# Query, key and value projections of an attention layer merged into 512-column products

## The chip, the cores and the metric

The kernel runs on one core of one Trainium2 chip. The metric is the device time of one execution in microseconds. Engines are named as in the profile: PE (TensorE), DVE (VectorE), ACT (ScalarE), POOL (GpSimd), and SP's queue, which issues the transfers.

## What is computed

One inference step of a two-layer encoder trunk for 640 tokens (a prompt of 512, and 8 running streams of 16 new tokens each) with 1024 features. Layer 0 mixes tokens by gating and convolution, layer 1 by an attention with forget values and RMS-normed queries and keys; each is followed by a convolutional feed-forward network (FFN). The change lies in layer 1's attention:

```python
def _fox_project(x, w_in, b_f, q_norm, k_norm):
    z = x @ w_in
    q, k, v, f = jnp.split(z, [D_C, 2 * D_C, 3 * D_C], axis=-1)
    q = _rmsnorm(q.reshape(b, t, C_HEADS, C_HEAD_DIM), q_norm)
    k = _rmsnorm(k.reshape(b, t, C_HEADS, C_HEAD_DIM), k_norm)
    v = v.reshape(b, t, C_HEADS, C_HEAD_DIM)
    logf = jax.nn.log_sigmoid((f + b_f).astype(jnp.float32))
    return q, k, v, logf

def _fox_attend(q, k, v, dq, dk, q_pos, k_pos):
    s = jnp.einsum('bthd,bshd->bhts', q, k, preferred_element_type=jnp.float32) * (C_HEAD_DIM ** -0.5)
    s = s + jnp.swapaxes(dq, 1, 2)[..., :, None] - jnp.swapaxes(dk, 1, 2)[..., None, :]
    s = jnp.where(k_pos[None, :] <= q_pos[:, None], s, NEG_INF)
    p = jax.nn.softmax(s, axis=-1)
    return jnp.einsum('bhts,bshd->bthd', p.astype(v.dtype), v)
```

There are 16 heads of 64 features. The prompt attends to itself, each stream to 256 cached keys and its own 16. The outputs go through `w_out`. Keys and values are outputs of the step as well.

## The kernel before

Tokens and weights are float32. To keep that accuracy, every factor is split into a high and a low float32r part (`weights`, L88 and L89, for weights; `split` and `prep` for activations), and a product is three matmuls: high by high, low by high, high by low. The weights come in units of 128 x 1024 through a pool `wts` with three buffers each for the raw unit and its two parts.

In time, the stages are the first mixer (to some 220 us), FFN 0 (to 679.6 us), the attention (to 1039 us), the rest of its output projection with the next norm (to 1076 us) and FFN 1.

The attention works through four groups of four heads, each group as two pairs. For a group g, `project` (L484) makes queries, keys and values, tokens on partitions, in a z tile of five token blocks each. Per kind there are two weight units, and each token block takes 8 chunks x 3 matmuls of 256 columns (L507), two blocks side by side in one 512-column PSUM tile `pj` of a pool with two buffers. ACT evacuates each block with the token's norm factor (L510). For queries and keys, ACT squares (L515), DVE reduces to sums per head (L516), POOL takes the power -1/2 (`rstd_of`, L151 and L152), then DVE scales (L519, z x ss) and, for keys, multiplies by the norm's weights (L521). `decay` makes the forget values and their sums; it stands after the queries of group 0.

For each pair, `operands` (L537 to L552) transposes queries and keys on PE, and ACT and DVE make high and low parts of them, `qa` and `ka` with `qb` and `kb`; halves of these are copied by transfers on SP's queue (L545, L548). `prompt_block` takes 128 queries of one head: scores `sc` on PE (L569, L570), mask on DVE (L571), `softmax` (maximum on DVE, L589; exponential on ACT, L591; reciprocal and division on DVE, L592 and L594), transposes (L576), copies `u` (DVE L579, ACT L581) and value products `pv` (L583). Blocks 3 to 0 of both heads alternate; `streams_pair` (L634 to L670) is laid between them, four per group. The PSUM pools are pj 2, sc 2, pt 3 and pv 1 buffers. The output projection `po` of the first six (for blocks 6 and 7 of the output, four) head pairs uses the same two pj buffers and stands in the program behind the last group; for it, `split` makes `sh` and `sl` from the finished heads.

The order of instructions on each engine isn't that of the program. A list scheduler (`schedule_with_timeline_sim=True`) sets it when the kernel is built, from the program's order, the dependences, the rotation of the pools and its own estimates of durations. It takes projections of a later group between the attention work of an earlier one. What is shown below as the order is what it put out.

## Time and profile before

| what | value |
|---|---|
| median of 3 runs | 1533.6 us (1533.28 to 1536.43) |
| span of the profiled execution, first to last instruction | 1531.9 us |
| the profiled execution's own device time | not given by the page; the median is 1.7 us above its span |
| PE busy | 1517.8 us, 99%, 11008 matmuls |
| DVE busy | 899.1 us, 59% |
| ACT busy | 559.4 us, 37% |
| POOL busy | 237.4 us, 15% |
| mean granted clock of PE | 1.000 |
| HBM read and written | 125.41 and 11.54 MB |

"Busy" is the time in which an instruction of the engine ran; a matmul's recorded duration is longer than the distance to the next one's start, since matmuls are pipelined, so costs on PE are taken from distances of starts. The chain of waits is the work that ended last, followed back from the last instruction. A row of a group names line, engine and operation, output <- inputs, shape and count; behind the bar stand busy us and mean ns of one, then the engine's idle time before it and what ended it. A row of stretches gives busy us and count for each engine.

### The profile page before, as it was taken

What the parts mean: (1) busy time and instruction counts of PE and PEld (TensorE: products, weight loads), DVE (VectorE), ACT (ScalarE), POOL (GpSimd) and SP (SyncE); (2) the same over time, 40 slices, a digit from 0 to 9 for tenths busy, and PEclk for the clock granted to TensorE, in tenths of its full rate; (3) what the DMA queues carried; (4) which work ended last, traced back from release to release, by engine and by line L of the source; (5) the groups of instructions that cost most, each with busy time, mean ns of one, the idle gap of its engine ahead of it and who ended that gap; (6) DMA issues with size and microseconds to landing.
All of it is one profiled execution on the core that took longest, in us unless ns stands there. A gap on an engine that the chain in (4) does not pass through costs nothing.

```text
span 1531.9 us, 26648 instructions
## 1 busy us (share of the span) xinstructions
PE 1517.8 (99%) x11008; PEld 1473.5 (96%) x11008; DVE 899.1 (59%) x1541; ACT 559.4 (37%) x918; POOL 237.4 (15%) x281
## 2 busy tenths in 40 slices
PE   8999999999999999999999999999999999999999
PEld 6999999999999999999989888888999999999998
DVE  6545437644653655675676766768765466365463
ACT  5422334322322322345545454535432233133231
POOL 5000122201210201143111111003221021021010
PEclk9999999999999999999999999999999999999999
DMA  6222212222223222243544343523222222321313
GB/s 226 77 82 73 77 56 85 68 81 85 62 64 95 64 66 93 62 156 103 180 128 136 122 123 104 183 60 107 83 60 76 87 67 57 98 73 53 107 47 106
DMA packets 52296, 142.90 MB, mean 93 GB/s; under 512 B 6656, under 2 KB 13744, under 8 KB 52048
## 3 DMA queue, kind: packets, MB, share of 16 engines
q1 hardware_dynamic: 45424, 133.79, 28.6%
q10 hardware_dynamic: 6752, 7.41, 1.4%
q8 instruction: 87, 1.43, 0.4%
q14 instruction: 33, 0.27, 0.1%
HBM read 125.41 MB, written 11.54 MB: 89 GB/s over the span
## 4 chain that ended last, share of the span: by engine, by line
PE 96%; DVE 2%; issue 1%; ACT 1%; DMA 0%; POOL 0%; SPq 0%; DVEq 0%; ACTq 0%
PE mm L109 71%; PE pj L507 10%; PE pv L583 3%; PE po L109 2%; PE pt L576 1%; PE mm L239 1%; PE pt L662 1%; PE sc L569 1%; DVE hl L132 1%; PE sc L570 1%; DVE wlo L89 1%; PE scs L641 1%; PE pt L537 1%; PE pt L655 0%; PE scs L634 0%
## 5 line engine op out<-in xcount | busy, mean ns | idle before, releaser
L88 ACT CAST whi<-raw 128x1024 fp32r<-128x1024 f32 (+4 forms) x222 | 207.6, 937 | 494.6 <-PE mm L109 426.1
L109 PE MATMUL mm<-hl,whi 128*128 128x320 f32 x1664 | 379.4, 309 | 0.5 <-DVE hl L132 0.5
L109 PE MATMUL mm<-hh,whi 128*128 128x320 f32 x1664 | 379.8, 309 | 0.0
L109 PE MATMUL mm<-hh,wlo 128*128 128x320 f32 x1664 | 379.2, 309 | 0.0
L109 PEld LDWEIGHTS mm<-hl,whi 128*128 128x128 f32 x1664 | 278.2, 188 | 0.7 <-DVE hl L132 0.7
L109 PEld LDWEIGHTS mm<-hh,whi 128*128 128x128 f32 x1664 | 278.2, 188 | 0.1
L109 PEld LDWEIGHTS mm<-hh,wlo 128*128 128x128 f32 x1664 | 278.0, 188 | 0.0
L89 DVE TENSOR_TENSOR wlo<-raw,whi 128x1024 fp32r<-128x1024 f32 (+4 forms) x222 | 245.5, 1107 | 33.3 <-ACT whi L88 33.0
L109 PE MATMUL mm<-sh,wlo 128*128 128x320 f32 x866 | 197.2, 309 | 1.3 <-DVE wlo L89 1.3
L109 PE MATMUL mm<-sl,whi 128*128 128x320 f32 x866 | 197.2, 309 | 0.0
L109 PE MATMUL mm<-sh,whi 128*128 128x320 f32 x866 | 196.2, 309 | 0.0
L202 POOL COPY so<-zp 128x18 f32<-128x18 f32 x88 | 89.4, 1016 | 570.4 <-DVE zp L191 570.4
L190 DVE TENSOR_TENSOR zp<-mm,rb 128x512 f32<-128x512 f32 x88 | 60.9, 692 | 195.8 <-PE mm L109 195.8
L209 DVE TENSOR_TENSOR x<-mm,x 128x640 f32<-128x640 f32 x79 | 65.0, 823 | 185.6 <-PE mm L109 185.6
L198 DVE SCALAR_TENSOR_TENSOR t<-zp,cst,t 128x656 f32<-128x656 f32 x184 | 165.1, 900 | 10.3 <-ACT t L196 5.6
L109 PEld LDWEIGHTS mm<-sh,wlo 128*128 128x128 f32 x866 | 144.6, 188 | 1.6 <-DVE wlo L89 1.6
L109 PEld LDWEIGHTS mm<-sl,whi 128*128 128x128 f32 x866 | 144.8, 188 | 0.0
L109 PEld LDWEIGHTS mm<-sh,whi 128*128 128x128 f32 x866 | 144.4, 188 | 0.2 <-issue 0.2
L507 PE MATMUL pj<-wlo,hh 128*128 128x256 f32 x480 | 137.7, 287 | 0.7 <-DVE wlo L89 0.7
L507 PE MATMUL pj<-whi,hh 128*128 128x256 f32 x480 | 137.7, 287 | 0.0
L507 PE MATMUL pj<-whi,hl 128*128 128x256 f32 x480 | 137.5, 287 | 0.0
L507 PEld LDWEIGHTS pj<-wlo,hh 128*128 128x128 f32 x480 | 91.6, 191 | 2.8 <-issue 1.6
(188 smaller groups left out, 1691.3 us busy)
## 6 DMA issues: line engine op xcount, KB each, us to landing
...
```

What stands on the lines that cost most here:

```text
L88: nc.scalar.copy(out=hi[:, c], in_=raw[:, c])
L89: nc.vector.tensor_tensor(out=lo[:, c], in0=raw[:, c], in1=hi[:, c].bitcast(F32), op=ALU.subtract)
L109: nc.tensor.matmul(outs[h], lhsT=l, rhs=r[:, h * HT:(h + 1) * HT], start=start and k == 0, stop=stop and k == 2)
L132: nc.vector.scalar_tensor_tensor(out=lo, in0=x, scalar=gs, in1=hi.bitcast(F32), op0=ALU.mult, op1=ALU.subtract)
L190: nc.vector.tensor_tensor(out=op, in0=a[:, 0:TP], in1=b[:, 0:TP], op=ALU.mult)
L198: nc.vector.scalar_tensor_tensor(out=cv[:, 0:CW], in0=zp[:, i:i + CW], scalar=w[:, i:i + 1], in1=cv[:, 0:CW], op0=ALU.mult, op1=ALU.add)
L202: self.nc.gpsimd.tensor_copy(out=out.rearrange("p (s c) -> p s c", c=2), in_=zp[:, 496:ZW].rearrange("p (s c) -> p s c", c=18)[:, :, 16:18])
L209: self.nc.vector.tensor_tensor(out=x, in0=ps[:, C0:C0 + T], in1=x, op=ALU.add)
L239: nc.tensor.matmul(pvs[tb], lhsT=l[:, tb * P:(tb + 1) * P], rhs=r[:, (kc % 2) * 512:(kc % 2 + 1) * 512], start=kc == 0 and k == 0, stop=kc ...
L507: nc.tensor.matmul(out[tb], lhsT=l[:, tb * P:(tb + 1) * P], rhs=r[:, c:c + 256], start=kc == 0 and i == 0, stop=kc == 7 and i == 2)
L537: nc.tensor.transpose(t[:, tb * P:(tb + 1) * P], z[i][:, tb, pair * P:(pair + 1) * P], k.ident)
L583: nc.tensor.matmul(ov[64 * hh:64 * hh + 64, i * P:n], lhsT=z[2][:, j, (2 * pair + hh) * 64:(2 * pair + hh) * 64 + 64], rhs=u[:, j * P:(j + ...
```

## The change

Queries and keys of a group are projected together, 256 + 256 columns side by side (`project_qk`), and values for two groups at once (`project_v`, called for groups 0 and 2). Every projection matmul is now 512 columns wide and each token block takes a whole pj tile; there are four weight units for such a product instead of two. In group 0 the token blocks go in pairs over the weights, as before for queries only. `decay` comes after queries and keys of group 0. One z tile holds queries and keys: z x ss is one DVE instruction for both, and the key norm's product takes half of that tile. The pool of weights has four buffers for the split parts and three for the raw unit, as before; the square has one buffer. The constants `w_qk` and `w_vc` replace `w_c`, with the same bytes. Comments are dropped, and the scratch for dynamic DMAs is set.

```diff
-        self.wp = pool(ctx, "wts", bufs=3)
+        self.wp = pool(ctx, "wts", bufs=4)
...
-        raw = self.wp.tile([P, 1024], F32, tag="raw", name=self.nm("raw"))
+        raw = self.wp.tile([P, 1024], F32, tag="raw", name=self.nm("raw"), bufs=3)
...
-    def project(self, g, h, first, after_q=None):
+    def walk(self, us, n, h, pairs):
+        k, nc = self.k, self.nc
+        out = [None] * 5
+        for tbs in ([(0, 1), (2, 3), (4,)] if pairs else [(tb,) for tb in range(5)]):
+            for tb in tbs:
+                out[tb] = self.pj.tile([P, 512], F32, tag="pj", name=k.nm("pj"))
+            for kc in range(8):
+                wh, wl = us[kc // n]
+                hh, hl = h[kc]
+                c = (kc % n) * 512
+                for tb in tbs:
+                    for i, (l, r) in enumerate(((hh, wh), (hl, wh), (hh, wl))):
+                        nc.tensor.matmul(out[tb], lhsT=l[:, tb * P:(tb + 1) * P], rhs=r[:, c:c + 512],
+                                         start=kc == 0 and i == 0, stop=kc == 7 and i == 2)
+            for tb in tbs:
+                yield tb, out[tb]
+
+    def project_qk(self, g, h):
+        us = [k.weights(io["w_qk"][g, u]) for u in range(4)]
+        zt = self.zp.tile([P, 5, 512], F32, tag="qk", name=k.nm("z"), bufs=2)
+        ss = self.zp.tile([P, 40], F32, tag="ss", name=k.nm("ss"))
+        for tb, o in self.walk(us, 2, h, g == 0):
+            nc.scalar.activation(out=zt[:, tb, :], in_=o, func=AF.Copy, scale=self.rt[:, tb:tb + 1])
+            sq = self.zp.tile([P, 512], F32, tag="sq", name=k.nm("sq"), bufs=1)
+            nc.scalar.activation(out=sq, in_=zt[:, tb, :], func=AF.Square)
+            s = ss[:, tb * 8:tb * 8 + 8]
+            nc.vector.reduce_sum(out=s, in_=sq.rearrange("p (h d) -> p h d", d=64), axis=AX.X)
+            k.rstd_of(s, s, 1.0 / 64)
+        zh = zt.rearrange("p t (h d) -> p (t h) d", d=64)
+        nc.vector.tensor_tensor(out=zh, in0=zh, in1=ss.unsqueeze(2).broadcast_to([P, 40, 64]), op=ALU.mult)
+        zk = zt[:, :, 256:512].rearrange("p t (h d) -> p t h d", d=64)
+        nc.vector.tensor_tensor(out=zk, in0=zk, in1=self.cst[:, O_KN:O_KN + 64].unsqueeze(1).unsqueeze(1).broadcast_to([P, 5, 4, 64]), op=ALU.mult)
...
+        return zt[:, :, 0:256], zt[:, :, 256:512]
+
+    def project_v(self, gg, h):
+        us = [k.weights(io["w_vc"][gg, u]) for u in range(4)]
+        zt = self.zp.tile([P, 5, 512], F32, tag="v", name=k.nm("z"), bufs=2)
+        for tb, o in self.walk(us, 2, h, False):
+            nc.scalar.activation(out=zt[:, tb, :], in_=o, func=AF.Copy, scale=self.rt[:, tb:tb + 1])
...
+    v = []
     for g in range(4):
-        z = at.project(g, h, g == 0, decay if g == 0 else None)
+        qk = at.project_qk(g, h)
+        if g == 0:
+            decay()
+        if g % 2 == 0:
+            v += at.project_v(g // 2, h)
+        z = qk + (v[g],)
...
-    nc = bacc.Bacc("TRN2", target_bir_lowering=False, num_devices=1)
+    nc = bacc.Bacc("TRN2", target_bir_lowering=False, num_devices=1, dynamic_dma_scratch_size=1024)
```

The lines of the attention behind `project` move by six in the listing (L569 is L575 in the changed kernel, L546 is L552, L571 is L577, L109 stays).

The order of the instructions moves. Groups are counted from 0. DVE at the start of group 2, from the copy of the streams' keys to the mask of the first score; `qb` and `ka` are operands of group 2, the squares' sums `ss` and `z` belong to group 3. Before:

```order
L604 COPY kts_9141<-pt_9136 128x256
L89 TENSOR_TENSOR wlo_9891<-raw_9889,whi_9890 128x1024
L546 SCALAR_TENSOR_TENSOR qb_9165<-pt_9153,qn_6341,qa_9163 64x512
L549 TENSOR_TENSOR ka_9164<-pt_9158,ka_9164 64x512
L546 SCALAR_TENSOR_TENSOR qb_9177<-pt_9153,qn_6341,qa_9175 64x512
L549 TENSOR_TENSOR ka_9176<-pt_9158,ka_9176 64x512
L516 TENSOR_REDUCE ss_9862<-sq_9863 128x4
L516 TENSOR_REDUCE ss_9862<-sq_9868 128x4
L151 TENSOR_SCALAR ss_9862<-ss_9862 128x4 x2
L571 TENSOR_TENSOR sc_9188<-sc_9188,mskb 128x128
```

In the changed kernel:

```order
L610 COPY kts_8565<-pt_8560 128x256
L513 TENSOR_REDUCE ss_9170<-sq_9321 128x8
L151 TENSOR_SCALAR ss_9170<-ss_9170 128x8
L552 SCALAR_TENSOR_TENSOR qb_8589<-pt_8577,qn_6341,qa_8587 64x512
L516 TENSOR_TENSOR z_9169<-z_9169,ss_9170 128x2560
L555 TENSOR_TENSOR ka_8588<-pt_8582,ka_8588 64x512
L98 TENSOR_TENSOR sl_9342<-x_77,sh_9341 128x640
L552 SCALAR_TENSOR_TENSOR qb_8601<-pt_8577,qn_6341,qa_8599 64x512
L518 TENSOR_TENSOR z_9169<-z_9169,atcst 128x5x256
L555 TENSOR_TENSOR ka_8600<-pt_8582,ka_8600 64x512
L577 TENSOR_TENSOR sc_8612<-sc_8612,mskb 128x128
```

The scaling z x ss of group 3, now 128x2560, and the key norm's product stand between the operands of group 2's first pair; before, these four operands followed each other.

PE at the same place, from the transposes of group 2's operands (`pt` from `z`). Before, where 57 matmuls of the projection follow before the first score `sc`:

```order
L537 MATMUL pt_9158<-cst,z_8836 128x128 x4
L507 MATMUL pj_9734<-whi_9728,hl_6173 128x256
L507 MATMUL pj_9734<-wlo_9729,hh_6172 128x256
L507 MATMUL pj_9734<-whi_9728,hh_6218 128x256
L507 MATMUL pj_9734<-whi_9728,hl_6219 128x256
L507 MATMUL pj_9734<-wlo_9729,hh_6218 128x256
L507 MATMUL pj_9734<-whi_9728,hh_6264 128x256
```

In the changed kernel, to that score:

```order
L543 MATMUL pt_8577<-cst,z_8244 128x128 x4
L589 MATMUL pv_7970<-u_8216,z_6734 64x128
L543 MATMUL pt_8582<-cst,z_8244 128x128 x4
L109 MATMUL po_9944<-sl_9338,whi_9939 128x320
L109 MATMUL po_9945<-sl_9338,whi_9939 128x320
L109 MATMUL po_9944<-sh_9337,wlo_9940 128x320
L109 MATMUL po_9945<-sh_9337,wlo_9940 128x320
L109 MATMUL po_9944<-sh_9341,whi_9939 128x320
L109 MATMUL po_9945<-sh_9341,whi_9939 128x320
L575 MATMUL sc_8612<-ka_8588,qa_8587 128x512
L576 MATMUL sc_8612<-kb_8590,qb_8589 128x512
L640 MATMUL scs_8638<-sr,sl 128x272
```

Six matmuls of the output projection stand there now, and no projection of a later group: all of these come earlier in the changed order.

PE in the second pair of group 2, from the scores on: `pj` is the projection, `pt` transposes, `pv` value products, `sc` scores. Before:

```order
L507 MATMUL pj_10073<-wlo_10061,hh_6080 128x256
L655 MATMUL pt_9607<-cst,pp_9599 128x128 x2
L569 MATMUL sc_9652<-ka_9291,qa_9290 128x256
L570 MATMUL sc_9652<-kb_9293,qb_9292 128x256
L507 MATMUL pj_10073<-whi_10060,hh_6126 128x256
L655 MATMUL pt_9607<-cst,pn_6353 128x128
L569 MATMUL sc_9670<-ka_9303,qa_9302 128x256
L570 MATMUL sc_9670<-kb_9305,qb_9304 128x256
L507 MATMUL pj_10073<-whi_10060,hl_6127 128x256
L507 MATMUL pj_10073<-wlo_10061,hh_6126 128x256
L507 MATMUL pj_10073<-whi_10066,hh_6172 128x256
L507 MATMUL pj_10073<-whi_10066,hl_6173 128x256
```

In the changed kernel:

```order
L575 MATMUL sc_8826<-ka_8588,qa_8587 128x256
L576 MATMUL sc_8826<-kb_8590,qb_8589 128x256
L582 MATMUL pt_8749<-cst,p_8742 128x128 x3
L589 MATMUL pv_8611<-u_8753,z_8428 64x128 x3
L661 MATMUL pt_8781<-cst,pp_8773 128x128 x2
L661 MATMUL pt_8781<-cst,pn_6351 128x128
L575 MATMUL sc_8844<-ka_8600,qa_8599 128x256
L576 MATMUL sc_8844<-kb_8602,qb_8601 128x256
L575 MATMUL sc_8862<-ka_8588,qa_8587 128x128
L576 MATMUL sc_8862<-kb_8590,qb_8589 128x128
L668 MATMUL pt_8781<-cv_8760,up_8785 32x128 x8
L668 MATMUL pt_8781<-z_8428,up_8785 32x128 x4
```

The projections between scores and the work behind them are gone here. In the changed order, 8 matmuls of `po` are all that stands between group 2's fourth score block and group 3's first score.

## Rows read from the trace of the kernel before

**Rows 1.** The head of the page, the granted clock in 40 slices, and the chain's shares by engine.

```profile
span 1531.9 us, 26648 instructions
PE 1517.8 (99%) x11008; PEld 1473.5 (96%) x11008; DVE 899.1 (59%) x1541; ACT 559.4 (37%) x918; POOL 237.4 (15%) x281
...
PEclk9999999999999999999999999999999999999999
...
PE 96%; DVE 2%; issue 1%; ACT 1%; DMA 0%; POOL 0%; SPq 0%; DVEq 0%; ACTq 0%
```

**Rows 2.** The chain of waits: start us, us, engine, line, count.

```profile
20.40 2.72 PE mm L239 x12
...
40.55 19.50 PE mm L109 x133
...
679.94 5.52 PE pj L507 x46
```

**Rows 3.** Timeline of PE, a projection run's end: start us, us, engine, line.

```profile
768.94 0.28 PE L507 MATMUL pj<-whi,hl 128*128 128x256 f32 x1
769.15 0.32 PE L583 MATMUL pv<-u,z 128*64 128x128 f32 x1
```

**Rows 4.** Stretches: length; busy us (count) of PE, PEld, DVE, ACT, POOL; clock; DMA share; GB/s.

```profile
690.00:722.00 32.00, 31.28 (x252) 31.08 (x251) 17.88 (x34) 19.20 (x34) 11.29 (x11) 1.00 0.34 110
818.92:897.33 78.41, 78.41 (x715) 68.90 (x713) 52.38 (x150) 38.03 (x97) 10.21 (x11) 1.00 0.40 127
897.33:977.13 79.80, 79.80 (x711) 70.19 (x709) 57.96 (x158) 40.40 (x101) 9.75 (x10) 1.00 0.41 134
977.13:1039.80 62.67, 62.07 (x533) 52.05 (x532) 42.64 (x136) 23.20 (x65) 0.27 (x4) 1.00 0.27 81
1025.15:1039.80 14.65, 14.05 (x120) 11.76 (x117) 10.24 (x39) 6.80 (x21) 0.00 (x0) 1.00 0.06 22
```

**Rows 5.** Busy time by stretch, of line L507 alone: PE, weight loads, clock, DMA.

```profile
818.92:897.33 78.41, 49.97 (x362) 45.59 (x360) 1.00 0.40 127
...
889.30:897.33 8.03, 6.91 (x57) 6.89 (x57) 1.00 0.81 258
```

**Rows 6.** Timelines of PE, DVE, SP's queue, PE: start us, us, engine, line [idle before].

```profile
889.68 0.98 PE L537 MATMUL pt<-cst,z 128*128 128x128 f32 x7
...
891.12 0.74 DVE L546 SCALAR_TENSOR_TENSOR qb<-pt,qn,qa 64x512 fp32r<-64x512 f32 x1 [2.10 <-ACT qa L544]
891.89 0.69 DVE L549 TENSOR_TENSOR ka<-pt,ka 64x512 fp32r<-64x512 f32 x1
...
891.73 0.55 SPq L548 DMA_DIRECT2D kb<-ka  x1
...
1025.15 0.44 PE L569 MATMUL sc<-ka,qa 128*128 128x384 f32 x1
...
1039.08 0.99 PE L109 MATMUL mm<-sh,whi 128*128 128x320 f32 x5
```

**Rows 7.** Groups of DVE, then ACT, 679 to 1040 us: count | busy, mean ns | idle before.

```profile
L571 DVE TENSOR_TENSOR sc<-sc,mskb 128x128 f32<-128x128 f32 x64 | 18.6, 296 | 28.4 <-PE sc L570 28.2
...
L592 DVE RECIPROCAL l<-l 128x1 f32<-128x1 f32 x80 | 12.8, 160 | 8.1 <-ACT p L591 6.7 <-ACT pp L591 0.7
L519 DVE TENSOR_TENSOR z<-z,ss 128x1280 f32<-128x1280 f32 x8 | 11.9, 1490 | 1.9 <-POOL ss L152 1.6
...
L579 DVE COPY u<-pt 128x256 f32<-128x256 f32 x16 | 6.8, 424 | 13.8 <-PE pt L576 12.9 <-PE sc L570 0.9
...
L594 DVE TENSOR_SCALAR p<-p,l 128x128 f32<-128x128 f32 x16 | 4.6, 286 | 0.5
L589 DVE TENSOR_REDUCE m<-sc 128x1 f32<-128x128 f32 x16 | 4.4, 286 | 0.2
...
L670 DVE COPY o<-pt 64x32 f32<-64x32 f32 x16 | 2.3, 182 | 0.1
...
L591 ACT ACTIVATE p<-sc,m 128x128 f32<-128x128 f32 x16 | 5.8, 367 | 7.7 <-DVE m L589 6.1 <-DVE l L592 0.9 <-PE pt L576 0.7
```

More of the change, by code (lines that the diff above doesn't have):

```diff
@@ L482, in decay @@
         nc.sync.dma_start(out=f(self.sl[2:18]), in_=f(sr))
-    def project(self, g, h, first, after_q=None):
-        k, nc, io = self.k, self.nc, self.io
-        z = []
-        for kind in range(3):
-            if kind == 1 and after_q is not None:
-                after_q()
-            us = [k.weights(io["w_c"][g, kind, u]) for u in range(2)]
-            zt = self.zp.tile([P, 5, 256], F32, tag="qk" if kind < 2 else "v", name=k.nm("z"), bufs=3 if kind < 2 else 2)
-            z.append(zt)
-            bank, out = [], []
-            for tb in range(5):
-                if tb % 2 == 0:
-                    bank.append(self.pj.tile([P, 512], F32, tag="pj", name=k.nm("pj")))
-                out.append(bank[tb // 2][:, (tb % 2) * 256:(tb % 2) * 256 + 256])
-            walk = [(0, 2), (1, 3), (4,)] if first and kind == 0 else [(tb,) for tb in range(5)]
-            for tbs in walk:
-                for kc in range(8):
-                    wh, wl = us[kc // 4]
-                    hh, hl = h[kc]
-                    c = (kc % 4) * 256
-                    for tb in tbs:
-                        for i, (l, r) in enumerate(((hh, wh), (hl, wh), (hh, wl))):
-                            nc.tensor.matmul(out[tb], lhsT=l[:, tb * P:(tb + 1) * P], rhs=r[:, c:c + 256],
-                                             start=kc == 0 and i == 0, stop=kc == 7 and i == 2)
-            for tb in range(5):
-                nc.scalar.activation(out=zt[:, tb, :], in_=out[tb], func=AF.Copy, scale=self.rt[:, tb:tb + 1])
-            if kind < 2:
-                ss = self.zp.tile([P, 20], F32, tag="ss", name=k.nm("ss"))
-                for tb in range(5):
-                    sq = self.zp.tile([P, 256], F32, tag="sq", name=k.nm("sq"))
-                    nc.scalar.activation(out=sq, in_=zt[:, tb, :], func=AF.Square)
-                    nc.vector.reduce_sum(out=ss[:, tb * 4:tb * 4 + 4], in_=sq.rearrange("p (h d) -> p h d", d=64), axis=AX.X)
-                    k.rstd_of(ss[:, tb * 4:tb * 4 + 4], ss[:, tb * 4:tb * 4 + 4], 1.0 / 64)
-                zh = zt.rearrange("p t (h d) -> p (t h) d", d=64)
-                nc.vector.tensor_tensor(out=zh, in0=zh, in1=ss.unsqueeze(2).broadcast_to([P, 20, 64]), op=ALU.mult)
-                if kind == 1:
-                    nc.vector.tensor_tensor(out=zh, in0=zh, in1=self.cst[:, O_KN:O_KN + 64].unsqueeze(1).broadcast_to([P, 20, 64]), op=ALU.mult)
-            if kind:
-                nc.scalar.dma_start(out=io["o_kv"][kind - 1, :, :, 256 * g:256 * g + 256].rearrange("t p c -> p t c"), in_=zt)
-        return z
@@ L830, in _layout @@
     wc = a["w_in_c"][0]
-    d["w_c"] = con(wc[:, :3072].reshape(2, 4, P, 3, 4, 256).transpose(4, 3, 0, 2, 1, 5)).reshape(4, 3, 2, P, 1024)
+    rows = lambda w: con(w.reshape(4, 2, P, 512).transpose(0, 2, 1, 3)).reshape(4, P, 1024)
+    grp = lambda kind, g, n: wc[:, 1024 * kind + n * g:1024 * kind + n * g + n]
+    d["w_qk"] = np.stack([rows(np.concatenate([grp(0, g, 256), grp(1, g, 256)], 1)) for g in range(4)])
+    d["w_vc"] = np.stack([rows(grp(2, g, 512)) for g in range(2)])
     wf = np.zeros((1024, P), f)
```

4 lines of the change are left out of this document (added).

## The prediction

> **What bounds the kernel now.** I read four views in this order. The head of the page first: of a span of 1531.9 us TensorE (PE) is busy 1517.8, its granted clock reads 9 tenths or more in all 40 slices (the upper level, 2.4 GHz), and the chain that ended last is 96% PE [rows 1]. So a microsecond is gained only where PE needs less of its own time, and lost only where PE must wait. The table of stretches says that this holds in the attention too: two whole groups show PE busy 78.41 of 78.41 and 79.80 of 79.80 us, the last one 62.07 of 62.67, while VectorE (DVE) is busy 52.38, 57.96 and 42.64 [rows 4]. Third, the chain of waits gives what a matmul costs when PE runs without a gap: 512 columns 2.72/12 = 226.7 ns, 256 columns 5.52/46 = 120.0 ns, 320 columns 19.50/133 = 146.6 ns [rows 2]. Between 256 and 512 that is 0.417 ns a column and 13.3 ns for each matmul, whatever its width. Last, where the projections lie: 362 of them stand between the score products of one group, about 43.4 us of its 78.41 [rows 5]. The remaining 35.0 us are attention work, which always waits for a softmax on DVE and ScalarE (ACT). PE shows no idle because projections cover every such wait. That cover is what the change moves.
>
> **The change, part by part.**
>
> *Wider matmuls.* 4 groups x 3 kinds x 5 token blocks x 8 chunks x 3 products = 1440 matmuls of 256 columns become 720 of 512. 1440 x 120.0 = 172.8 us; 720 x 226.7 = 163.2 us. **Saved 9.6 us**, all of it PE's own time. The row of 512 columns comes from the same kind of product (split parts, three matmuls to a product) of the first mixer, so I take it as it stands; the bounds are 0 (a wide one costs twice 120.0) and 11.0 (the narrow ones at 121 in the mean, as their runs are broken up).
>
> The Trainium skill ("TensorE: Matmul & The Clock Gate", section "Back-to-back issue gap") gives for a warm matmul the columns at 2.4 GHz plus some 2.5 ns, which would be 109.2 and 215.8 ns, and the saving an estimated 1.9 us. The trace does not agree: it shows 13.3 ns on top at both widths, and the measurement decides.
>
> *Fewer changes between projection and attention.* In a run of projections the starts lie 0.12 us apart; at the change to a value product they lie 0.21 apart [rows 3], 0.09 more. By the order there are 63 fewer returns to projections (134 to 71), but only 12 fewer changes from a projection to a value product (36 to 24). 12 x 0.09 = **1.1 us saved**; bounds 0, and 63 x 0.09 = 5.7 if every kind of change costs as much.
>
> *Where the projections go.* Keys now come with the queries, values for two groups at once, so the scheduler, which fills PE's waits from later code, meets the work in larger lumps and earlier. By the order it has used up all projections before the third group (group 2, counted from 0) starts: between first score products there were 47.2, 43.2, 44.5 and 27.3 us of cover (at the prices above), now 57.1, 54.2, 8.8 and 25.2. Group 2 keeps only 60 output projections of 0.147 us, 52 of them before its fourth score block; from there to group 3's first score lie 13 of its 16 blocks and 3 of 4 stream pairs with 8 small matmuls between them. Four costs follow.
>
> (a) *The border from group 1 to group 2.* Before, 57 projections lie in the 8.03 us between the last key transposes and the first score [rows 5]. Now there are six output projections, 0.88 us. DVE does qb at 891.12 and ka until 892.58 right behind it [rows 6], some 1.9 us after the transposes, the last of which end at 890.66. In the new order the query-key scaling z x ss stands between the two, 128x2560 where 128x1280 took 1490 ns [rows 7]; twice that, less the overlap, is 2.8 to 2.9 us. So the first score comes 1.9 + 2.8 = 4.7 us after the transposes; less 0.9 of cover, **3.8 us are lost**. Bounds: 0, if DVE's queue runs ahead and has the scaling behind it when the transposes end, and 6.0, if the mean square it multiplies by (reduction, POOL's power) is late as well. Queued behind it are ka, both operands of the second head and the first mask, and PE itself.
>
> (b) *The bare stretch.* The last five blocks of before are the nearest rows: 1025.15 to 1039.08 [rows 6], 13.9 us, in which 24 output projections (29 less the five of the next stage) stood, 3.5 us; 10.4 us for five blocks with their stream parts, 2.08 each, only 0.6 of it idle [rows 4]. 13 x 2.08 = 27.0 us, about PE's own work there (35.0 x 13/16 = 28.4, less the transposes and stream scores issued ahead). On top come two waits with no cover. One is for the next group's operands: 1.9 us after the transposes as in (a), and a DMA on SP's queue that brings half of them, issued until 892.28, 1.6 us after the transposes [rows 6], whose landing no row gives: I take 3.0 in all. The other is the softmax tail of the last block: mask 0.30, maximum 0.29, exponential 0.37, reciprocal 0.16, division 0.29, copy 0.42 [rows 7], with PE's transposes 2.0. **5.0 us lost.** DVE is close behind: its rows of the four groups, twelve of the blocks (from the masks' 18.6 us to the copies' 6.8) and seven of the streams (to 2.3 us for the last copies) [rows 7], add to 25.5 us a group for blocks and 8.9 for streams, so 20.7 + 6.7 in the stretch, and 33.1 with the operands of two pairs (2 x 2 x 1.43, rows of (a)) by durations: about as much as the 27.0 + 5.0 us that I give the stretch, so DVE would be nearly full there. Bounds: 0, as PE was busy 14.05 of 14.65 in the last five blocks, and 13, the rival below.
>
> (c) *Group 3* keeps 25.2 instead of 27.3 us of cover while its softmax chain is unchanged; it had 0.6 us idle [rows 4], so less cover shows in full at worst: **2.5 us** with the wait at its own border, bounds 0 and 5.
>
> (d) *The start.* Four weight units must be split, not two, before the first block closes, and the forget chain moves behind queries and keys. Before, PE was idle 0.7 us in the 32 us around that chain [rows 4]; the cover ahead of it is now 120 wide matmuls, 27 us, for 120 narrow ones, 14. **0.5 us**, bounds 0 and 2.
>
> Nothing each: weights are as many bytes on SP's queue, and the fourth buffer lets them come earlier; 20 reductions of 128x512 for 40 of 128x256 and 20 POOL powers for 40 lie beside PE work wherever cover is left; the evacuations, half as many and twice as wide, sit on ACT at 38 to 40 us of 78 to 80 [rows 4]. If that cover goes, they are part of (a) and (b), the only places where it does. The smaller DMA scratch and the dropped comments move no instruction.
>
> **The sum.** 9.6 + 1.1 = 10.7 us saved, 3.8 + 5.0 + 2.5 + 0.5 = 11.8 lost: +1.1 on the span, 1533.0. The median of the runs, 1533.6, lies 1.7 above the profiled span of 1531.9, so about **1535 us**: no change that this kernel's measurement can tell, which needs 0.2%, 3.1 us.
>
> **The rivals.**
>
> *Slower: the bare softmax does not overlap.* If in the stretch (b) each round of two heads waits for its own softmax before the next scores issue (the score pool has two buffers, and DVE runs the blocks in one file), a block costs what the chain costs, not what PE costs: DVE's 33.1 us bind, plus one exposed chain of 2.0 and the operands' 4.7 make 40 instead of 27: 13 lost. With (a) 3.8, (c) 2.5 and (d) 0.5 the losses are 19.8, net +9.1, about 1543 us. For it: DVE's sum is above PE's there; before 1035 the last five blocks still had 3.5 us of cover. Against: only 0.6 us idle at the very end [rows 4]. It decides from 9 us lost in (b) on. Chance 0.33.
>
> *Slower: a wide matmul costs as much as two narrow ones here* (240 ns): then 0 is saved, and 11.8 lost against 1.1 saved give +10.7, 1544 us. Only the rule named above comes near it, by a smaller part for each matmul; by its 1.9 us the time would be an estimated 1542. Against: 226.7 ns over twelve matmuls in a row [rows 2]. Chance 0.03.
>
> *Slower: PE's clock falls in the bare stretch.* At half the clock its 27 us of work would take up to twice as long, some +20 us. No stretch of the trace shows a fall, the one with PE idle 0.7 in 32 us included [rows 4]; in the bare stretch it would still be busy over 80%. Chance 0.02.
>
> *Faster: the stretch covers itself.* Four products of two heads, the stream pairs and the next pair's transposes interleave as in the last 14 us, at 0.6 idle per 14.65 [rows 4]; then (b) is 1.5, (a) 2.0 as DVE runs ahead, (c) and (d) 1.3 together. Losses 4.8, net -5.9: about 1527.7 us. For it: PE's 99% with a DVE already at 66 to 73% in the groups; against: that was with cover. Chance 0.22.
>
> **How the numbers follow.** No measurable change 0.40 is the forecast; faster 0.22; slower 0.33 + 0.03 + 0.02 = 0.38. The range of the forecast's own case is 1530.5 to 1537. The full range reaches to the faster case's middle and over the slower one's bound: 1528 to 1547; what it leaves out is half of the faster case and the falling clock, under 0.2.
>
> **What would show it.** PE matmuls of 512 columns every 227 ns in runs of the projection; a PE row with idle of 3 to 4 us before the first score of group 2, put down to ka; in the stretch behind it the first slices of the attention where PE is under 95%, DVE over 80%, with idle before value products and scores put down to DVE; no such idle in groups 0 and 1. I am wrong if PE is busy over 98% through group 2 (the cover was not needed), if the stretch takes over 36 us (the chain binds), or if new idle stands in groups 0 and 1, where I have put none.

## The result, and the profile after

The changed kernel takes 1541.4 us (1539.4 to 1542.4), the kernel before 1534.5 beside it: ratio 1.0041, 95% interval [1.0028, 1.0055]. It is slower by 0.4%, where no measurable change was forecast (1535); the range and its slower side (0.38) held it. The profiled execution took 1539.4 us, its span 1537.6, against 1531.9 [rows 1]. It is the quickest of the four executions of the changed kernel: its mean granted clock is 0.996, that of the other three 0.994.

The head of the page and the chain's shares:

```profile
span 1537.6 us, 25069 instructions
...
PE 1513.6 (98%) x10288; PEld 1432.3 (93%) x10288; DVE 894.8 (58%) x1497; ACT 555.6 (36%) x868; POOL 227.4 (15%) x261
...
PE 95%; DVE 2%; issue 1%; ACT 1%; DMA 0%; SPq 0%; DVEq 0%; ACTq 0%
```

PE is busy 4.2 us less in a longer span; its share fell to 98%. The stretches from first score to first score, groups 0 to 3 (columns as in [rows 4]):

```profile
745.60:835.94 90.34, 90.34 (x606) 69.67 (x604) 57.64 (x150) 45.09 (x96) 15.00 (x9) 1.00 0.42 134
835.94:928.30 92.36, 88.90 (x599) 68.09 (x597) 58.16 (x148) 41.61 (x95) 10.08 (x6) 1.00 0.43 141
928.30:982.44 54.14, 47.42 (x412) 35.63 (x413) 42.30 (x131) 25.77 (x70) 0.00 (x0) 0.94 0.43 128
982.44:1045.52 63.08, 61.33 (x514) 49.98 (x513) 43.25 (x138) 23.39 (x66) 0.27 (x4) 0.97 0.26 80
```

Group 0 of the kernel before:

```profile
738.95:818.92 79.97, 79.97 (x747) 71.88 (x746) 53.92 (x155) 40.39 (x102) 10.35 (x11) 1.00 0.45 144
```

Groups 0 and 1 hold the projections that were pulled ahead, 90 and 92 us long (80 and 78 before), and PE is full in group 0. Group 2 is 54.1 us long and PE busy 47.4 of it; before, it was 79.8 us long and full [rows 4]. New is the clock: 0.94 and 0.97 in the last two. From the first projection to the next stage's first matmul the attention takes 365.9 us (679.6 to 1045.5), before 359.3. That is 6.6 us more; the whole span is 5.7 longer, as the rest of the program took 0.9 less in these two executions. Where the waits are, from the view of waits on PE:

```profile
PE po L109 <- ACT sh L97: 4.4, 2, 3.0
PE sc L575 <- DVE ka L555: 2.1, 1, 2.1
PE pv L589 <- ACT u L587: 1.4, 3, 0.6
...
PE po L109 <- DVE x L786: 1.0, 1, 1.0
PE sc L575 <- ACT p L597: 0.9, 1, 0.9
PE scs L640 <- ACT p L597: 0.6, 1, 0.6
```

The columns are total, count and longest, in us. At the border from group 1 to 2 PE waits 1.4 for ACT's `sh`, 2.1 for `ka` and, after the first scores, 1.0 for DVE; at the border from 2 to 3 it waits 3.0. The clock around the two borders (the column before the last two):

```profile
925.00:930.00 5.00, 2.26 (x21) 1.12 (x21) 4.87 (x5) 1.87 (x3) 0.00 (x0) 0.91 0.38 87
930.00:935.00 5.00, 3.97 (x19) 3.04 (x12) 4.94 (x9) 1.86 (x4) 0.00 (x0) 0.50 0.79 166
935.00:940.00 5.00, 5.00 (x33) 4.88 (x33) 3.40 (x11) 1.06 (x3) 0.00 (x0) 0.91 0.59 216
980.00:985.00 5.00, 2.95 (x25) 2.14 (x25) 3.14 (x6) 3.44 (x7) 0.00 (x0) 0.87 0.44 102
985.00:990.00 5.00, 5.00 (x28) 4.55 (x28) 4.37 (x12) 1.73 (x5) 0.00 (x0) 0.79 0.64 206
```

Twice the clock's distance from 1, times the length, gives the time at the lower level (1.2 GHz): 0.9, 5.0, 0.9, 1.3 and 2.1 us, 10.2 in all. The output projection's matmuls show both levels:

```profile
935.03 0.47 PE L109 MATMUL po<-sl,whi 128*128 128x320 f32 x1
935.29 0.47 PE L109 MATMUL po<-sh,wlo 128*128 128x320 f32 x1
...
936.59 0.31 PE L109 MATMUL po<-sh,whi 128*128 128x320 f32 x1
936.74 0.31 PE L109 MATMUL po<-sl,whi 128*128 128x320 f32 x1
```

Starts lie 0.26 us apart at the lower level, 0.15 at the upper. So half of the 10.2 us, less 0.5 for the 1.0 in which PE waited anyway, is an estimate of **4.6 us by which the clock lengthened PE's work**; by the two distances just named, 0.12 of each 0.27 us, it is 4.1. Less than that was lost, as `e3_dummy` and `e4_ztb` show below.

Adding up the distances from each matmul's start to the next one's, idle apart, gives where the attention's time went:

| us from start to start | before | after |
|---|---|---|
| projections `pj` (1440 and 720) | 182.8 | 169.5 |
| output projection `po` (252 each) | 39.0 | 43.5 |
| transposes and stream values `pt` | 44.3 | 49.8 |
| scores `sc`, `scs` | 42.2 | 44.2 |
| value products `pv` | 41.6 | 38.8 |
| idle of PE | 1.3 | 12.0 |

The forget values' projection and the token norms, 8.0 us in both, are left out. The projections gave 13.3 us and the value products 2.8; idle took 10.7, and the same matmuls of `po`, `pt` and scores took 12.0 us longer. That sums to the 6.6 us that the attention lost. A part of the 12.0 is waiting too. A wait counts as idle only from the recorded end of the matmul ahead of it, and a transpose is recorded with 0.27 us though four of them in a row start some 0.1 us apart. Before, 3 matmuls stand ahead of an idle stretch, now 23, 15 of them transposes and stream values; at 0.2 us each that is an estimate of 4 us.

### The profile page after: what moved, and what is told of

Read it like the earlier page. It is cut to its first block, busy times and chain, and to the rows that moved or that the text cites. A ratio compares the mean times of both kernels' runs of the same rounds, so it can differ in the third digit from the quotient of the medians.

```text
span 1537.6 us, 25069 instructions
## 1 busy us (share of the span) xinstructions
PE 1513.6 (98%) x10288; PEld 1432.3 (93%) x10288; DVE 894.8 (58%) x1497; ACT 555.6 (36%) x868; POOL 227.4 (15%) x261
## 4 chain that ended last, share of the span: by engine, by line
PE 95%; DVE 2%; issue 1%; ACT 1%; DMA 0%; SPq 0%; DVEq 0%; ACTq 0%
PE mm L109 71%; PE pj L497 11%; PE po L109 2%; PE pv L589 2%; PE pt L582 1%; PE mm L239 1%; PE pt L668 1%; PE sc L575 1%; DVE wlo L89 1%; PE sc L576 1%; PE scs L647 1%; DVE hl L132 1%; PE pf L109 0%; PE pt L543 0%; PE pt L661 0%
## 5 line engine op out<-in xcount | busy, mean ns | idle before, releaser
L109 PE MATMUL mm<-hl,whi 128*128 128x320 f32 x1664 | 379.5, 309 | 1.1 <-DVE hl L132 1.1
L109 PE MATMUL mm<-hh,whi 128*128 128x320 f32 x1664 | 379.7, 309 | 0.0
L109 PE MATMUL mm<-hh,wlo 128*128 128x320 f32 x1664 | 379.3, 309 | 0.0
L109 PEld LDWEIGHTS mm<-hl,whi 128*128 128x128 f32 x1664 | 278.3, 188 | 1.3 <-DVE hl L132 1.3
L109 PEld LDWEIGHTS mm<-hh,whi 128*128 128x128 f32 x1664 | 278.2, 188 | 0.1
L109 PEld LDWEIGHTS mm<-hh,wlo 128*128 128x128 f32 x1664 | 278.1, 188 | 0.0
L89 DVE TENSOR_TENSOR wlo<-raw,whi 128x1024 fp32r<-128x1024 f32 (+4 forms) x222 | 245.9, 1110 | 28.7 <-ACT whi L88 28.1
L109 PE MATMUL mm<-sl,whi 128*128 128x320 f32 x866 | 197.3, 309 | 0.0
L109 PE MATMUL mm<-sh,wlo 128*128 128x320 f32 x866 | 197.3, 309 | 0.0
L109 PE MATMUL mm<-sh,whi 128*128 128x320 f32 x866 | 196.4, 309 | 0.0
L202 POOL COPY so<-zp 128x18 f32<-128x18 f32 x88 | 86.0, 977 | 571.1 <-DVE zp L191 571.1
L109 PEld LDWEIGHTS mm<-sh,wlo 128*128 128x128 f32 x866 | 144.8, 188 | 0.0
L109 PEld LDWEIGHTS mm<-sl,whi 128*128 128x128 f32 x866 | 144.8, 188 | 0.0
L109 PEld LDWEIGHTS mm<-sh,whi 128*128 128x128 f32 x866 | 144.5, 188 | 0.2 <-issue 0.2
L497 PE MATMUL pj<-whi,hh 128*128 128x512 f32 x240 | 95.4, 398 | 0.1
L497 PE MATMUL pj<-whi,hl 128*128 128x512 f32 x240 | 94.5, 394 | 0.0
L497 PE MATMUL pj<-wlo,hh 128*128 128x512 f32 x240 | 93.8, 394 | 0.0
L196 ACT ACTIVATE t<-zp,cst 128x656 f32<-128x656 f32 x92 | 77.7, 846 | 36.1 <-DVE zp L191 36.1
```

Source lines behind the costliest of these rows:

```text
L89: nc.vector.tensor_tensor(out=lo[:, c], in0=raw[:, c], in1=hi[:, c].bitcast(F32), op=ALU.subtract)
L109: nc.tensor.matmul(outs[h], lhsT=l, rhs=r[:, h * HT:(h + 1) * HT], start=start and k == 0, stop=stop and k == 2)
L196: nc.scalar.activation(out=cv[:, 0:CW], in_=zp[:, 2:ZW], func=AF.Copy, scale=w[:, 2:3])
L202: self.nc.gpsimd.tensor_copy(out=out.rearrange("p (s c) -> p s c", c=2), in_=zp[:, 496:ZW].rearrange("p (s c) -> p s c", c=18)[:, :, 16:18])
L497: nc.tensor.matmul(out[tb], lhsT=l[:, tb * P:(tb + 1) * P], rhs=r[:, c:c + 512], start=kc == 0 and i == 0, stop=kc == 7 and i == 2)
```

## The experiments

Two explanations stood at first. **Cover**: the wide products save what they should, and the loss comes from where the projections now stand. **Form**: longer pieces on DVE and ACT, and a whole bank for each block, cost more than narrow ones. Later runs split cover into the *border* between groups and the *stretch* of blocks. Ratios are to the kernel before, run beside each.

**Cut the wide products in two.** `e2_narrow`:

```diff
-            for kc in range(8):
...
-                c = (kc % n) * 512
...
-                        nc.tensor.matmul(out[tb], lhsT=l[:, tb * P:(tb + 1) * P], rhs=r[:, c:c + 512],
...
+            for e in (0, 256):
+                for kc in range(8):
...
+                    c = (kc % n) * 512 + e
...
+                            nc.tensor.matmul(out[tb][:, e:e + 256], lhsT=l[:, tb * P:(tb + 1) * P], rhs=r[:, c:c + 256],
```

> The changed kernel with each product of 512 columns made as two halves of 256 columns one after the other: 1440 matmuls again, everything else of the change kept. By the order group 2 keeps 26.7 us of cover (8.8 before). Cover theory with a saving of the wide matmuls of 10 to 13 us: the projections cost 10 to 13 more, the idle of group 2 and the clock falls (8.8 + 4.3 us) mostly go: 1538 to 1544 us, with PE nearly without idle in group 2. Rival (a wide matmul saves nothing here, the order alone costs): 1528 to 1533 us. Rival (the wide form of the pieces on DVE and ACT costs): idle stays, over 1548 us.

Measured: 1545.8 us, ratio 1.0075 [1.0063, 1.0088], 4.3 us above the changed kernel. The projections take 181.2 us from start to start, 11.7 more, and idle falls from 12.0 to 8.8. So the wide products do save about 12 us. In the chain of waits the longest runs of projections, of the changed kernel and of this one:

```profile
728.94 16.82 PE pj L497 x74
```

```profile
723.83 23.99 PE pj L498 x200
```

16.82/74 = 227.3 ns and 23.99/200 = 120.0 ns, within 1 ns of the prices of [rows 2]. The time is 2 us above the range for cover. Group 2 was to be nearly without idle and kept 6.6 us of it (6.7 in the changed kernel), with three times the cover: 3.0 at the border from group 2 to 3, where the clock fell for 6.8 us. What went is the idle of group 1, 3.5 us.

**Scale each block by itself.** `e4_ztb` takes the long piece out of DVE's queue:

```diff
-        zh = zt.rearrange("p t (h d) -> p (t h) d", d=64)
-        nc.vector.tensor_tensor(out=zh, in0=zh, in1=ss.unsqueeze(2).broadcast_to([P, 40, 64]), op=ALU.mult)
+            zb = zt[:, tb, :].rearrange("p (h d) -> p h d", d=64)
+            nc.vector.tensor_tensor(out=zb, in0=zb, in1=s.unsqueeze(2).broadcast_to([P, 8, 64]), op=ALU.mult)
```

> The changed kernel with the scaling of queries and keys done for each token block (five pieces of 128x512) instead of once for all (128x2560). By the order only one piece of some 0.7 us stands between the first two operands of group 2 on DVE, where 2.8 us stood; cover in group 2 is the same 8.8 us. If the scaling's place on DVE costs what the prediction's term (a) says: the wait for ka before group 2's first score falls from 2.1 us to under 0.5, the time by 2 us to 1539.5, and by 2 to 3 more (1537) if the clock then stays up at this border. Rival (ACT's part for the output projection, 1.4 us, and the operands' transfers end last there anyway): the wait changes its name, 1541 us.

Measured: 1536.1 us, 1.0012 [1.0002, 1.0021], 5.3 us gained. DVE at the border from group 1 to 2, in the changed kernel and in this one:

```profile
924.06 0.74 DVE L552 SCALAR_TENSOR_TENSOR qb<-pt,qn,qa 64x512 fp32r<-64x512 f32 x1 [1.46 <-ACT qa L550]
924.73 2.81 DVE L516 TENSOR_TENSOR z<-z,ss 128x2560 f32<-128x2560 f32 x1
927.57 0.68 DVE L555 TENSOR_TENSOR ka<-pt,ka 64x512 fp32r<-64x512 f32 x1
```

```profile
923.66 0.74 DVE L552 SCALAR_TENSOR_TENSOR qb<-pt,qn,qa 64x512 fp32r<-64x512 f32 x1 [1.38 <-ACT qa L550]
924.33 0.68 DVE L516 TENSOR_TENSOR z<-z,ss 128x512 f32<-128x512 f32 x1
925.04 0.69 DVE L555 TENSOR_TENSOR ka<-pt,ka 64x512 fp32r<-64x512 f32 x1
```

The scaling behind `qb` took 2.81 us and `ka` came after it; now 0.68. The wait for `ka` is gone; 0.9 us for `sh` and 0.75 for a transfer of `qa` remain, 1.7 of idle in group 1 instead of 3.5. From first score to first score group 1 got only 0.7 us shorter, but it holds six projections more (232 instead of 226, 1.4 us): 2.1 us of its own. So term (a)'s wait is shown in its place and was worth about its length. Group 0, with four projections less (0.9 us), got 2.4 us shorter, and group 3 1.4, group 2 0.1 with the same cover. So some 3 us more were gained in groups 0 and 3, where 0.2 of idle went. That speaks for a part of "form", a long piece in DVE's queue that delays what stands behind it; no run takes it apart.

The clock did not stay up. At the first border of this run:

```profile
925.00:930.00 5.00, 3.99 (x25) 2.33 (x25) 4.66 (x8) 1.60 (x4) 0.00 (x0) 0.73 0.80 223
930.00:935.00 5.00, 4.68 (x20) 4.42 (x20) 4.15 (x11) 1.84 (x5) 0.00 (x0) 0.58 0.67 243
```

It fell behind the two waits of 0.9 and 0.75 us, and at both borders together it was low for 10.2 us, as in the changed kernel. So the time came out below what was forecast for a clock that stays up (1537), without that gain. What the clock costs shows in the eleven executions of this one program. Their mean clock lies between 0.999 and 0.991 and their span between 1531.5 and 1539.0 us, and the longer ones are the ones with the lower clock: 7.5 us for 24.6 us more at the lower level, 0.3 us for each. By that rate the changed kernel's 10.2 us cost an estimated 3 us, if nothing else differs between these executions; only one of them has a trace. One program doesn't get the same falls in every execution.

**Added work in the waits.** `e3_dummy`, which computes 24 products more whose result is not used:

```diff
+        if g > 1 and pair == 0:
+            t = self.ptile()
+            a = self.h0
+            for i in range(12):
+                nc.tensor.matmul(t, lhsT=a[:, 0:P], rhs=a[:, 0:512], start=i == 0, stop=i == 11)
...
+        at.h0 = h[0][0]
```

> The changed kernel with 12 more matmuls of 512 columns (2.7 us, their result is not used) right behind the key transposes at the starts of groups 2 and 3, where PE waits 3.5 and 3.0 us in the changed kernel; the order is otherwise the same. Clock theory (part of the loss is that PE's clock falls to its lower level after these waits): the granted clock stays at 1.00 around both borders, the waits shrink to under 1 us, and the time falls by 3 to 4 us to about 1537.5 although 5.4 us of work were added. If only the waits cost: 1541 us, unchanged, as the added work lies in them. If the added work isn't hidden: 1543 to 1547.

Measured: 1543.5 us, 1.0060 [1.0046, 1.0074].

```profile
930.00:935.00 5.00, 2.76 (x29) 2.09 (x30) 4.91 (x9) 0.83 (x1) 0.00 (x0) 0.99 0.78 243
935.00:940.00 5.00, 5.00 (x25) 4.91 (x24) 3.15 (x11) 2.08 (x5) 0.00 (x0) 0.67 0.40 139
...
985.00:990.00 5.00, 4.52 (x37) 3.24 (x36) 3.45 (x8) 1.35 (x3) 0.00 (x0) 1.00 0.68 191
```

At the first border the added 2.7 us hid (first score at 928.93, 928.30 without): of the two waits there, 1.4 and 2.1 us, only one of 1.5 is left, and the clock stays up to 934.9 us (0.50 from 930 to 935 in the changed kernel). It falls later, behind a wait of 2.2 us for DVE, to 0.67 from 935 to 940. At the second border the added matmuls waited for their own buffer and came behind 1.7 us of idle, so they were not hidden: the score moved from 982.44 to 985.98. The clock stays at 1.00 there (0.87 and 0.79 in the changed kernel). `po` takes 41.5 us instead of 43.5. That puts the time in the third case.

The mean clock of this run's five executions is 0.996 to 0.999, of the changed kernel's four 0.994 to 0.996. So the falls go with PE's waits, and filling them with work of no use moves the falls; that idle PE is the cause is the nearest reading of this. The price stays an estimate. A part of the low-clock time cost nothing: from the first score to the next block of `po` it is 4.7 us in both kernels, as that block waits for DVE's `x` in both, 1.0 us with the clock low and 2.2 with it up. Taken off the 4.6 us, these 1.2 leave 3.4, near the 3 from the executions of `e4_ztb`.

**More cover for group 2.** `e1_qk1`:

```diff
-        zt = self.zp.tile([P, 5, 512], F32, tag="qk", name=k.nm("z"), bufs=2)
+        zt = self.zp.tile([P, 5, 512], F32, tag="qk", name=k.nm("z"), bufs=1)
```

> The changed kernel with one buffer instead of two for the query-key tile, so that queries and keys of the next group can only be evacuated once the group at work has made its operands. By the order this leaves 37.6, 54.4, 28.1 and 25.3 us of projections and output projections between the scores of groups 0 to 3 (the changed kernel: 57.1, 54.2, 8.8, 25.3). Cover theory (the loss comes from group 2 being left without projections): PE's idle in the attention falls from 12.0 to under 4 us, the clock stays at 1.00 at the borders, about 1526 us (1523 to 1530). Rival (the wide form itself costs: longer pieces on DVE and ACT, a whole bank for each token block): nothing of that changes, 1538 to 1543 us. A second rival is that one buffer makes PE wait for the operands: over 1543.

Measured: 1546.4 us, 1.0083 [1.0069, 1.0097], a miss of 20 us. Waits of PE from 800 to 850 us:

```profile
PE sc L575 <- DVE ka L555: 3.0, 1, 3.0
PE sc L575 <- ACT p L597: 2.0, 1, 2.0
PE pj L497 <- ACT z L509: 0.9, 1, 0.9
```

It moved the bare place: the border from group 0 to 1 now has no projections, and there stand 3.0 us for `ka`, 2.0 behind it and the fallen clock (0.50 from 825 to 830). The border from 2 to 3 keeps its 3.0. Idle in the attention rose from 12.0 to 17.3 us; group 2, with 28.1 us of cover instead of 8.8, has 7.9 of it (6.7 in the changed kernel). The time lies in the range of the second rival, whose own wait, of `pj` for ACT's `z`, is 0.9 us twice. Cover counted by group tells little; where in the group it stands does.

**Cover at the borders.** `e9_v1_only` is `e4_ztb` with one line, `e5_wide_v1` has two:

```diff
-        zt = self.zp.tile([P, 5, 512], F32, tag="v", name=k.nm("z"), bufs=2)
+        zt = self.zp.tile([P, 5, 512], F32, tag="v", name=k.nm("z"), bufs=1)
...
-    cut = [6, 6, 6, 6, 6, 4, 4, 4]
+    cut = [6, 6, 6, 6, 6, 6, 5, 5]
```

> All projections 512 wide as in the change, scaling for each token block (as in e4_ztb), one buffer for the values' tile and the output projection's last two blocks over five head pairs instead of four. By the order the projections of values for groups 2 and 3 now stand at the border from group 1 to 2 (16.3 us between the last transposes and the first score, 0.9 in the changed kernel), 4.0 us of output projection at the border from 2 to 3 (0.3 before); a bare stretch of 13 blocks is still there, in group 1 instead of 2. Border theory (what costs is a border between groups at which PE has nothing to do while operands are made, and the clock that falls there): the 5.0 us of waits at the borders of e4_ztb and some 2.5 us of clock go, 1529 us (1527 to 1531). Stretch theory (what costs is any long run of blocks without projections between them): 1534 to 1538 us, with the idle in group 1.

> e4_ztb with one buffer for the values' tile and nothing else: the half of e5_wide_v1 that moves the projections of values for groups 2 and 3 to the border from group 1 to 2 (16.3 us of cover there); the border from group 2 to 3 stays bare (0.3 us) and the output projection is cut as before. Border theory: the waits at the first border (2.0 us in e4_ztb) and its clock go, the 3.0 us wait at the second stays: 1533 us (1532 to 1534.5), so half-way between e4_ztb (1536.1) and e5_wide_v1 (1531.8). If the bare stretch, now in group 1, costs as much as before and the border nothing: 1536. If the output projection's cut made the whole gain of e5_wide_v1: 1536 too.

Measured: `e9_v1_only` 1534.8 us, 1.0005 [0.9996, 1.0013]; `e5_wide_v1` **1531.8 us, 0.9981 [0.9972, 0.9990]**, the only version below the kernel before. Groups 1 and 2 of `e5_wide_v1`:

```profile
834.80:901.60 66.80, 61.62 (x466) 46.43 (x466) 44.79 (x131) 30.40 (x76) 1.63 (x1) 0.97 0.41 127
901.60:978.90 77.30, 75.73 (x565) 60.63 (x564) 57.27 (x155) 39.11 (x90) 8.71 (x5) 1.00 0.48 159
```

Group 2 is nearly full again, at a clock of 1.00. The bare stretch went to group 1 with its idle: 5.2 of 66.8 us. Over the whole attention idle is 10.5 us in `e9_v1_only` and 8.9 in `e5_wide_v1`, against 9.4 in `e4_ztb`: nearly unchanged. What fell is the length of single waits (none above 1.1 us in `e5_wide_v1`; 3.0 in the other two) and the time at the lower clock in the attention, 3.4 us in both against 10.2. The attention of `e5_wide_v1` also holds 24 matmuls of `po` more (3.5 us) that stood in the next stage.

With the bare stretch went the longer distances. Transposes and stream values (`pt`) take 11.1 us in group 1 and 13.7 in group 2 of the changed kernel, and 13.5 and 12.5 in `e9_v1_only`, where group 1 is bare; the scores `sc` take 6.0 and 6.9, and 6.8 and 6.1. Before, it was 10.6 and 6.1 in both groups. No fall of the clock stands in these two groups of `e9_v1_only`. So a bare stretch costs some 3 us in such distances besides its idle.

Both theories hold in part: a bare stretch keeps its idle wherever it stands, and a bare border costs its wait and then the clock. `e9_v1_only` alone decides nothing, as it lies between the two theories' numbers (1533, 1536) and is not clear of `e4_ztb`. `e5_wide_v1` is clear of both of these runs, 0.8 us above the border theory's range and 2.2 below the stretch theory's.

**Values per group.** Three runs with values 256 wide again, from `e4_ztb`: one buffer for them (`e6_v_per_group`), one for queries and keys as well (`e7_v_per_group_qk1`), one for queries and keys alone (`e8_v_two_qk1`):

```diff
-        for tb, o in self.walk(us, 2, h, False):
+        for tb, o in self.walk(us, 4, h, False, 256):
...
-        if g % 2 == 0:
-            v += at.project_v(g // 2, h)
+        v += at.project_v(g, h)
```

> Queries with keys 512 wide, values per group 256 wide again (480 matmuls of 512 and 480 of 256: 6.4 us saved instead of 9.6), one buffer for the values' tile, scaling for each token block. By the order each border between groups has 5.8 us or more of projections, and the second pair of groups 0, 1 and 2 has a bare stretch of 8 to 11 blocks. Border theory: 1531 to 1535 us, clock 1.00 throughout. Stretch theory: three stretches at some 4 to 6 us each, 1540 to 1546 us.

> As e6_v_per_group with one buffer for the query-key tile too: queries and keys of the next group fall into the second half of a group. By the order every border has 5.8 us or more, group 2 has cover nearly throughout; bare are the first five blocks of group 0, four at the end of its second pair and eight in group 1's second pair. Border theory: 1530 to 1534 us. Stretch theory (some 0.5 us a bare block): 1536 to 1541 us. If the single buffer makes PE wait as in e1_qk1 (waits of 2 to 3 us at the border from group 0 to 1, although that border now has 5.8 us of cover): over 1541.

> As e7_v_per_group_qk1 with two buffers for the values' tile. By the order all borders have 6.6 to 10.9 us of cover, as before the change, and the second pairs are covered as before; bare are the first five or six blocks of groups 0, 1 and 2. Border theory: 1528 to 1532 us. Stretch theory: three stretches of five blocks at 2 to 4 us, 1535 to 1540 us.

Measured: 1540.9 us (1.0039 [1.0026, 1.0053]), 1551.7 (1.0107 [1.0093, 1.0121]) and 1542.4 (1.0050 [1.0037, 1.0063]). All are above the border theory's numbers; the first lies in the stretch theory's range, the second in that of the single buffer's wait (over 1541), the third above both theories. The clock did not stay at 1.00 in any of them (3.4, 17.1 and 6.8 us at the lower level in the attention). Single buffers made waits of their own, as in `e6_v_per_group`:

```profile
PE pj L497 <- ACT z L528: 4.2, 3, 1.7
```

At each border the projections fill both `pj` tiles and then wait for ACT, whose target is still being read by the old group. In the other two PE waits 3 us for a transfer of `qa` at the first score of all, and 2 us behind it; these two waits have the single buffer for queries and keys in common, and nothing shows how it causes them.

**Single blocks.** In `e10_blocks_8_8` and `e11_blocks_7_6` the tiles are one block each (`NQ` buffers for queries with keys, `NV` for values: 8 and 8, then 7 and 6):

```diff
-        zt = self.zp.tile([P, 5, 512], F32, tag="qk", name=k.nm("z"), bufs=2)
...
+            zt = self.zp.tile([P, 512], F32, tag="qk", name=k.nm("z"), bufs=NQ)
```

> All projections 512 wide; the tiles of queries with keys and of values are now one per token block, in pools of eight buffers each, so that the projections can run ahead by single blocks; scaling, key norm and the output of keys and values are done for each block (30 transfers for 6), the rest as in e5_wide_v1. By the order the cover is 30.8+22.7, 21.8+24.5, 6.2+7.6 and 18.8+10.6 us in the pairs of groups 0 to 3, 4.5 to 6.3 us at the borders, and 11 blocks instead of 16 lie in bare runs. If idle goes with bare borders and bare runs: PE's idle in the attention 4 to 6 us (8.9 in e5_wide_v1), 1528 to 1531 us. If the finer pieces on DVE and ACT's queue cost more than the cover brings: over 1533.

> As e10_blocks_8_8 with seven and six buffers. By the order the cover is 30.6+17.5, 15.0+21.5, 21.4+7.6 and 18.8+10.6 us, the same 4.5 to 6.3 us at the borders, 11 blocks in bare runs, the longest in the second pair of group 2. Cover that is spread evenly: 1528 to 1531 us, below e10_blocks_8_8 if group 2's own cover counts most. If the pool waits (PE waiting for ACT's evacuation, as in e1_qk1) come in: over 1534.

Measured: 1538.7 us (1.0033 [1.0021, 1.0046]) and 1541.4 (1.0047 [1.0035, 1.0060]). Both profiled executions are the longest of their runs (1544.5 of 1537.4 to 1544.5, and 1543.3 of 1541.0 to 1543.3), so their waits need not be in all. Idle is 10.1 and 12.5 us, of which one wait takes 3.4 and 6.4. In the second:

```profile
PE sc L590 <- ACT p L612: 6.4, 1, 6.4
```

The score waits 6.4 us for ACT's exponential, and the clock is 0.50 behind it. ACT stood ahead of that at the split of a weight unit, whose transfer (`raw` from `w_vc`) had not landed:

```profile
840.35 0.58 ACT L568 CAST ka<-pt 64x512 fp32r<-64x512 f32 x1
843.76 1.05 ACT L89 CAST whi<-raw 128x1024 fp32r<-128x1024 f32 x1 [2.83 <-DMA raw<-w_vc]
```

DVE's part of that unit (`wlo`, 844.84 to 846.07 us) then stood ahead of the maximum that the exponential needs. In `e10_blocks_8_8` ACT waits 4.0 us for a unit of the output projection, with the exponential next in its queue. So these waits are neither the pool's nor the finer pieces' of the expectations: weights came late, and the softmax stood behind them. Why they came late was not taken apart.

**One part alone.** `e12_before_wts4`, the kernel before with `bufs=4` for the split weights:

> The kernel before with one part of the change alone: four buffers instead of three for the weights' split parts. By the order its cover stays spread (17.8 to 26 us in each pair, borders 6.0 to 8.5 us). The prediction put this part at nothing: 1534 us, within 2 us of the kernel before. If the buffers alone make projections run ahead: over 1537.

Measured: 1536.5 us, 1.0010 [1.0002, 1.0019]: 2.4 us, so not quite the nothing of the prediction, and as much as a quarter of the change's loss. Whether the buffers cost the same within the change, no run shows.

## Why the prediction was right or wrong

- **Wider matmuls**, 9.6 us: right; the way back in `e2_narrow` costs 11.7. By the gap that the Trainium skill ("TensorE: Matmul & The Clock Gate", section "Back-to-back issue gap") gives for an isolated warm matmul, it would have been an estimated 1.9; the trace does not agree, with 227.3 and 120.0 ns.
- **Fewer changes**, 1.1 us: too low. The projections gave 13.3 us in all, 3.7 beyond the 9.6, and the value products 2.8; both together are over the term's bound of 5.7.
- **(a)**, 3.8 us: right in place and mechanism and nearly in size. The first score came 4.6 us after the transposes (4.7 forecast): 2.1 of idle for `ka` behind a scaling of 2.81 us, and 1.4 for `sh` ahead of it, where only one wait was foreseen. Another 1.0 came after it.
- **(b)**, 5.0 us: right that it costs, and nearly right in idle. From group 2's fourth block (947.4) to group 3's first score the stretch took 35.0 us, not 32: 5.7 of idle for the 5.0, and 29.3 of PE's own for the 27.0. The 3.0 us at the border came as priced, but not by the transfer that was named: it is ACT's queue.

```profile
978.10 0.68 ACT L550 ACTIVATE qa<-pt,qn 64x512 fp32r<-64x512 f32 x1 [0.55 <-PE pt L543]
978.68 0.57 ACT L567 COPY x<-pv 128x512 f32<-128x512 f32 x1
979.15 1.49 ACT L615 ACTIVATE qbd<-pt,qn 64x128 f32<-64x128 f32 x4
980.67 0.58 ACT L553 CAST ka<-pt 64x512 fp32r<-64x512 f32 x1
981.27 0.72 ACT L97 CAST sh<-x 128x640 fp32r<-128x640 f32 x1
```

Between `qa` and `ka` ACT copies the last outputs and makes four stream operands (0.57 and 1.49 us), then comes `sh`, for which PE's next matmul waits, with the scores behind it. DVE's part of `ka` ended at 981.96, `sh` at 981.99, so the scores had no earlier start without `sh`. The softmax tail is in the waits of 0.3 to 0.9 us above and in distances that no row calls idle.
- **(c)** 2.5 and **(d)** 0.5: high, by idle. Group 3's idle grew from 0.6 to 1.8 us, the start's fell from 0.7 to 0.1.
- **The sum** of losses was 11.8; idle grew by 10.7. The idle was foreseen. **The step that failed is the sum itself, in the term that it lacks**: what bare places do to PE's other work. `po`, `pt` and scores took 12.0 us longer, of which the larger savings on `pj` and `pv` gave back 5.4; that is what turned +1.1 into +6.6. An estimated 4.1 to 4.6 of the 12.0 is the clock. It was only a rival, at chance 0.02, placed in the stretch ("No stretch of the trace shows a fall"), and it fell behind both borders instead. The rest is in short attention matmuls without projections between, which start when their input comes: an estimated 4 us in the matmuls ahead of the 23 waits, and the distances moved with the bare stretch from group 2 to group 1 in `e9_v1_only`.
- **The slower rival** (chance 0.33, 1543 us) had the time nearly right, by luck and not by its mechanism: the rounds do overlap (35 us, not 40), and DVE, whose 33.1 us were to bind, was busy 28.4 us of the 35.0.
- **Nothing each**: the weights' buffers cost some 0.1%; ACT, costed at nothing, set the second border.

## What to carry to other kernels

Work that fills another stage's waits has a place as well as an amount. Before merging such work into larger pieces, list for each wait (border by border) what stands in it afterwards: here some 12 us of saving were lost to two bare borders and a bare stretch, and a version with the borders filled again (`e5_wide_v1`) kept 3. To a wait on PE add what the clock can take behind it; here waits of about 1 us, two of them close together, were followed by a fall too. One long instruction in an engine's queue, between two short ones that PE waits for, cost here about what it was longer (2.1 us). And one profile is one execution: `e4_ztb` varied by 7.5 us with its clock.

## What had not been expected

The clock fell behind waits of 1.4 and 2.1 us with two matmuls between (to 0.50 from 930 to 935 us), and behind one of 3.0. There it fell after the wait, when the work had begun again (1.00 from 980 to 982 us, 0.50 from 984 to 986); in `e2_narrow` it fell within the same wait (0.50 from 987 us, the wait ended at 988). In `e5_wide_v1` waits of 1.0 and 0.8 us in a stretch of short matmuls gave 0.85 and 0.81. The Trainium skill (the same page, section "Part 1: The HAM clock gate (the "warmup" mystery)") says that the low level is the state of rest, which activity releases; the trace agrees in that the changed kernel's clock fell at the two borders with waits and nowhere else in the attention, and came back to 1.00 while PE worked on without one, at 935.9 and 987.1 us.
